# One hybrid-attention encoder block on one core: stores moved to a second DMA queue, one weight load moved forward, filler matmuls redistributed, one bias tile shared

## The chip, the core and the metric

The kernel runs on one core of a Trainium2 chip. A core has TensorE (PE, matrix products), VectorE (DVE), ScalarE (ACT), GpSimd (POOL) and SyncE (SP), each with its own instruction stream that it works off in order, and 16 DMA engines that all of them share. Nearly every DMA here is issued by SP; a few are issued by ACT. The metric is the device time of one execution in microseconds (us). The kernel before takes 1512.31 us, the median of 3 runs that lie between 1511.23 and 1512.66 us.

## The reference

One sequence of 1024 positions with 1024 features goes through one block. What matters here is the mixing part:

```python
h = rmsnorm(x, g_mix[i]) * (1 + scale1) + shift1
proj = h @ w_in[i]
qa, ka, va, qb, kb, vb, ga, gb = jnp.split(proj, split_at, axis=-1)
oa = mixture_of_dilations(heads(qa, N_HEADS_DIL), heads(ka, N_HEADS_DIL), heads(va, N_HEADS_DIL), rel_bias)
ob = neighbourhood_attention_2d(heads(qb, N_HEADS_NA), heads(kb, N_HEADS_NA), heads(vb, N_HEADS_NA), na_rpb[i])
merged = jax.nn.sigmoid(ga) * ya + jax.nn.sigmoid(gb) * yb
```

There are 8 dilated heads (three window patterns, merged by their softmax denominators) and 8 heads of two-dimensional neighbourhood attention on a 16 x 64 grid. A query of the 2-D heads sees 8 rows and 16 columns, with the column window clamped at the edges:

```python
col_start = jnp.clip(cq - NA_COLS // 2, 0, GRID_W - NA_COLS)
bias = rpb[:, (dr + NA_ROWS_MAX - 1)[:, :, None, None], (dc + NA_COLS - 1)[None, None]]
```

The bias depends on the offset between query and key alone. Behind the mixers come the output projection, a gated ConvFFN and a last norm, none of which the change touches.

## The kernel before

Each float32 product is three TensorE products of a high and a low half (`hi`, `lo`). The program runs in stages:

- **Start to about 150 us.** The conditioning vector is multiplied with `w_ada` on VectorE (`row_pairs`, L655), `h` is made, and the value projections are computed for both branches (`v_wide`, L301). In the middle (the `step is None` branch, L728 to L741) the second half of the first query/key pair is projected; `qk_evict` (L372) splits the result into halves (ACT L366, DVE L368 and L370) and stores it to the scratch `q_scr` (L375); `va_chunks` (L412) reorders the values in HBM; `p_load(0)` (L708) fetches the two weight tiles of the first block product; `t_sums` forms operand sums on GpSimd. All this is written in a fixed order.
- **150 to 282 us, the product stage.** Seven pairs of query/key weight tiles go through a seven-product block scheme (`products`, L477; operands from `a_operands`, L428). Every result is split and stored to `q_scr` by `na_evict` (L379) or `qk_evict`: 28 stores of 512 KB. From here on a list scheduler that simulates the engines sets SP's order.
- **282 to 645 us, attention.** A table of slots says what is emitted where. Slots 0 to 63 hold the eight dilated heads (8 slots each), slots 64 to 95 start the eight 2-D heads (4 slots each, one of four blocks of 16 columns per slot, in the order 0, 3, 1, 2). A slot runs output products (`O`), transposes of the probabilities (`T`) and scores (`S`). Between them stand **fills**: a `next` of `fill_steps` (L1287) emits three 128x512 matmuls of the gate projections, which do not depend on attention. `n` of L1337 says how many fills a slot gets; `fill(1)` at L1334 runs ahead of slot 0. PE, ACT and DVE keep the order in which this is written; SP and GpSimd are ordered by the scheduler.
- **From 645 us on.** The rest of the fills, gating, output projection, FFN, final norm.

Names that the steps use: `qk_load` (L395) fetches one head's query and keys (`qs`, `ks`, `kl`) from `q_scr`; `dil_bias` and `bias` (L1212) fetch bias tiles into a ring of 4 buffers, the latter from `na_bias`, whose columns `na_col` holds per column block; `soft` in a head adds the bias and takes the row maximum on DVE (L874, L1237), then ACT takes the exponential (L875, L1239). A pair of dilated heads ends with its denominators: transposed (`turn`, L1113), stored to `st_scr` (`rows`, L1121), reloaded by nine small DMAs (`spread`, L1125 and L1129), and used on DVE (`factors`, L1135). For the last pair this falls into slots 65 to 68.

Of the kernel before, what the change touches and what calls it, by code (L numbers as in the profile page):

```python
# [29 lines left out]
def hybrid_encoder(tc, xT, c, w_ada, small, w_in, p1_bias, p23_bias, na_bias, ln2_mult, ident, w_br, w_out,  # L30
                   w_up, w_down, out):
    nc = tc.nc
    act, dve, pool, pe, sp = nc.scalar, nc.vector, nc.gpsimd, nc.tensor, nc.sync
# [5 lines left out]
    def f(ap):  # L39
        return ap.bitcast(FT)  # L40
# [331 lines left out]
    def qk_evict(pr, y, hf, p, tag):  # L372
        st = qkpool.tile([128, 2, 512], FR, name=tag)
        split_qk(y, (st[:, 0], st[:, 1]), p)
        sp.dma_start(q_scr[pr, 2 * y:2 * y + 2].rearrange("x p s -> p x s")[:, :, halves[hf]], f(st))  # L375

    na_st = {}

    def na_evict(pr, y, hf, p):  # L379
        first = (pr, y) not in na_st  # L380
        if first:
            na_st[pr, y] = [qkpool.tile([128, S], FR, name="qs") for _ in range(2)]
        st = na_st[pr, y]
        if y:
            split_qk(y, [t.rearrange("p (w t r) -> p r w t", w=16, t=16)[:, 2 * hf:2 * hf + 2] for t in st],
                     p.rearrange("p (r w t) -> p r w t", r=2, w=16))
        else:
            for r in range(2):
                split_qk(y, [t.rearrange("p (c w r t) -> p r c w t", c=4, w=16, r=4)[:, 2 * hf + r] for t in st],
                         p.rearrange("p (r w c t) -> p r c w t", r=2, w=16, c=4)[:, r])  # L390
        if not first:
            for x_, t in enumerate(na_st.pop((pr, y))):
                sp.dma_start(q_scr[pr, 2 * y + x_], f(t))

    def qk_load(head):  # L395
        pr, i = divmod(head, 2)
# [127 lines left out]
    with tc.manual_schedule(engines={e.engine for e in (sp, act, dve, pool, pe)}):  # L524
        x = [x_load(0)]
# [201 lines left out]
        for n, step in enumerate(v_steps[:10]):  # L727
            if step is None:  # L728
                for ks in (slice(0, 4), slice(4, 8)):
                    for hv in range(2):  # L730
                        v_split(v_raws[hv], (dve, pool), ks, v_w[hv])
                ps = [ps_g.tile([128, 512], FT, name="pj") for _ in range(2)]
                for k in range(KT):
                    for p, w in zip(ps, qk_w):
                        product(p, w, lambda k: h[1, k], ks=[k])
                for y in range(2):
                    qk_evict(0, y, 1, ps[y], "kl")
                va_chunks(slice(0, 512))
                raw[0] = p_load(0)
                t_sums()  # L740
                prep = [a_operands(raw.pop(0), 4, p_home, p_sts[0], spot=p_spot)]  # L741
            else:
                p = v_wide(*step[1:])
            row_pairs(done_rows, row_ends[n])
            if step is not None:
                for st, pp in zip(step[1:], p):
                    v_out(step[0], st, pp, queue=act)
            done_rows = row_ends[n]
            if n in PREP:
                next(prep[0])  # L750
# [425 lines left out]
                pool.tensor_tensor(dst, dst, src, OP.add)  # L1176
            sp.dma_start(o_scr[0][self.pr], u[1])

    na_col = [0, 576, 1344, 2112]

    class NaHead:
        def __init__(self, head, s0):
# [28 lines left out]

        def bias(self, cb):  # L1212
            kn = 48 * NA_NC[cb]
            bt = self.bt[cb] = sm_pool.tile([128, 896], FT, name="bias", bufs=4)
            sp.dma_start(bt[:, :2 * kn], na_bias[self.head][:, na_col[cb]:na_col[cb] + 2 * kn])

# [114 lines left out]

    att = contextlib.ExitStack()
    att.enter_context(tc.manual_schedule(engines={e.engine for e in (pe, act, dve)}))
    fill(1)  # L1334
    for s in range(102):
        n = 2 + s % 2 if s < 64 else 3 if s < 68 else 2 if s < 96 else 1
        settle()  # L1337
        run(slots[s]["first"])
        run(slots[s]["O"])
# [658 lines left out]
def _na_index():  # L1998
    parts = []
    p = np.arange(128)[:, None]  # L2000
    for cb in range(4):
        n = NA_NC[cb]
        for R in range(2):
            k = np.arange(48 * n)[None, :]
# [65 lines left out]
```

## Time and profile before

| what | value |
|---|---|
| median of 3 runs | 1512.31 us (1511.23 to 1512.66) |
| the profiled execution's own time | 1511.48 us |
| its span, first to last instruction | 1509.7 us |
| PE busy | 1455.2 us (96% of the span) |
| DVE / ACT / POOL busy | 965.4 / 790.3 / 839.3 us |
| mean granted TensorE clock | 0.984 of full |
| DMA moved | 244.28 MB, mean 162 GB/s |

The profile comes from one execution. Its page has the busy time of each engine, the span in 40 slices, the DMA queues, the chain of work that ended last and the costliest groups of instructions; further views of the same trace list waits by releaser, instructions in order of time, and busy times in chosen windows. In a row of the timeline stand start, duration, engine, line, operation, output and inputs, and in brackets how long the engine was idle before it and what released it. Matmuls are pipelined: the time that one costs is the distance between two starts, not its listed duration. An `SPq` or `ACTq` row is a DMA being issued. In a row of windows stand the length, the busy time of PE, PEld (weight load), DVE, ACT and POOL with the number of instructions, the granted TensorE clock, the DMA share and GB/s.

### The profile page before, as it was taken

How to read it: one execution, taken by the hardware profiler on the slowest of the kernel's cores; microseconds unless marked ns; L12 is line 12 of the kernel's file. 1: busy time of each engine (PE TensorE's matmuls, PEld its weight loads, DVE VectorE, ACT ScalarE, POOL GpSimd, SP SyncE). 2: the span in 40 equal slices, each digit the busy share in tenths (PEclk: the TensorE clock that was granted, in tenths of full speed). 3: DMA queues.
4: the chain of work that ended last, by engine and by line, in shares of the span. 5: the costliest groups of instructions: out<-in, count | busy, mean ns of one | idle time of the engine just before them, and what ended most of it. 6: DMA issues, size and time to landing. Idle time of an engine off the chain costs nothing.

```text
span 1509.7 us, 21346 instructions
## 1 busy us (share of the span) xinstructions
PE 1455.2 (96%) x7308; PEld 1228.7 (81%) x7308; DVE 965.4 (64%) x1809; ACT 790.3 (52%) x1479; POOL 839.3 (56%) x690
## 2 busy tenths in 40 slices
PE   9999999799999888999999999999999999999998
PEld 8877888588888777888888878888888888887788
DVE  7695544256666566756634898666666667887865
ACT  6624543177677556764335455444444446574542
POOL 4164675244342245532258848766666676988712
PEclk9999999899999989999999999999999999999999
DMA  9586255776666899958744412222222234632313
GB/s 369 201 311 240 98 181 179 206 187 168 177 182 174 252 218 258 245 192 278 251 131 154 140 56 99 84 84 84 84 84 84 84 119 140 213 125 81 99 49 112
DMA packets 131668, 244.28 MB, mean 162 GB/s; under 512 B 47940, under 2 KB 60868, under 8 KB 131524
## 3 DMA queue, kind: packets, MB, share of 16 engines
q1 hardware_dynamic: 129560, 239.97, 51.3%
q10 hardware_dynamic: 2000, 2.95, 0.5%
q8 instruction: 58, 0.95, 0.3%
q14 instruction: 50, 0.41, 0.1%
HBM read 188.74 MB, written 59.90 MB: 165 GB/s over the span
## 4 chain that ended last, share of the span: by engine, by line
PE 42%; DVE 4%; DMA 4%; POOL 3%; ACT 2%; issue 2%; SPq 0%; DVEq 0%; ACTq 0%; POOLq 0%
PE pj L495 10%; PE pj L496 10%; PE pj L497 10%; PE pj L86 4%; PE pj L84 4%; PE pj L85 4%; DMA oraw<-ob 1%; DMA oraw<-w_ada 1%; DMA wraw<-w_down 1%; POOL wlo L61 1%; POOL wsl L61 1%; ACT op L1518 1%; DVE big L460 0%; POOL big L442 0%; POOL big L441 0%
## 5 line engine op out<-in xcount | busy, mean ns | idle before, releaser
L61 POOL TENSOR_TENSOR wlo<-wraw,whi 128x512 fp32r<-128x512 f32 (+1 forms) x92 | 116.4, 1287 | 130.5 <-ACT whi L57 128.7
L495 PE MATMUL pj<-op,wsh 128*128 128x512 f32 x408 | 158.5, 390 | 1.4 <-ACT wsh L57 1.3
L496 PE MATMUL pj<-op,wsh 128*128 128x512 f32 x408 | 158.7, 389 | 0.4 <-DVE op L1489 0.4
L497 PE MATMUL pj<-op,wsl 128*128 128x512 f32 x408 | 157.3, 389 | 0.0
L61 POOL TENSOR_TENSOR wsl<-big,wsh 128x512 fp32r<-128x512 f32 (+1 forms) x86 | 111.5, 1319 | 44.5 <-ACT wsh L57 39.5
L84 PE MATMUL pj<-h,whi 128*128 128x512 f32 x272 | 118.0, 434 | 0.0
L85 PE MATMUL pj<-h,whi 128*128 128x512 f32 x272 | 109.0, 401 | 0.0
L86 PE MATMUL pj<-h,wlo 128*128 128x512 f32 x272 | 108.9, 400 | 0.0
L1699 DVE SCALAR_TENSOR_TENSOR big<-pj,sm,big 128x512 f32<-128x512 f32 (+2 forms) x183 | 94.9, 563 | 16.5 <-ACT big L1693 15.6
L889 DVE TENSOR_TENSOR tl<-T,th 128x512 fp32r<-128x512 f32 (+3 forms) x120 | 76.5, 650 | 24.9 <-ACT th L885 24.7
L495 PEld LDWEIGHTS pj<-op,wsh 128*128 128x128 f32 x408 | 76.6, 188 | 18.0 <-ACT wsh L57 2.2
L495 PE MATMUL pj<-op,whi 128*128 128x512 f32 x232 | 90.6, 391 | 0.3 <-ACT wc L501 0.3
L496 PE MATMUL pj<-op,whi 128*128 128x512 f32 x232 | 90.5, 390 | 0.2 <-DVE op L1519 0.2
L497 PE MATMUL pj<-op,wlo 128*128 128x512 f32 x232 | 90.3, 389 | 0.0
L496 PEld LDWEIGHTS pj<-op,wsh 128*128 128x128 f32 x408 | 76.6, 188 | 16.6 <-DVE op L1489 0.9
L497 PEld LDWEIGHTS pj<-op,wsl 128*128 128x128 f32 x408 | 76.6, 188 | 16.1 <-POOL wsl L61 0.2
L61 POOL TENSOR_TENSOR wsl<-wraw,wsh 128x384 fp32r<-128x384 f32 (+1 forms) x46 | 56.5, 1250 | 57.5 <-ACT wsh L57 53.2
L874 DVE CUSTOM_DVE_ANT_0 P<-S,bias 128x256 f32<-128x256 f32 x128 | 49.1, 420 | 60.3 <-PE S L1006 32.7
L57 ACT ACTIVATE whi<-wraw 128x1024 fp32r<-128x1024 f32 (+2 forms) x49 | 48.5, 994 | 66.7 <-PE pj L85 30.0
L875 ACT ACTIVATE P<-P,st 128x256 f32<-128x256 f32 x128 | 64.0, 504 | 26.5 <-DVE st L874 26.0
L1693 ACT ACTIVATE big<-pj,sm 128x512 f32<-128x512 f32 x61 | 47.0, 773 | 54.0 <-DVE pj L516 32.1
L516 DVE TENSOR_TENSOR pj<-pj,wc 128x512 f32<-128x512 f32 x40 | 27.8, 695 | 72.1 <-PE pj L497 72.1
(476 smaller groups left out, 4567.1 us busy)
## 6 DMA issues: line engine op xcount, KB each, us to landing
wada<-w_ada SPq DMA_DIRECT2D x31, 512.0 KB
qks<-qs SPq DMA_DIRECT2D x28, 512.0 KB
wraw<-w_in SPq DMA_DIRECT2D x26, 512.0 KB
big<-w_up SPq DMA_DIRECT2D x22, 512.0 KB
wraw<-w_up SPq DMA_DIRECT2D x22, 512.0 KB
big<-as SPq DMA_DIRECT2D x22, 512.0 KB
as<-big SPq DMA_DIRECT2D x21, 512.0 KB
qs<-qks SPq DMA_DIRECT2D x32, 256.0 KB
```

The source lines that it names most:

```text
L57: act.activation(hi, raw, AF.Copy)
L61: lo_eng.tensor_tensor(lo[:, i:i + step], raw[:, i:i + step], f(hi)[:, i:i + step], OP.subtract)
L84: pe.matmul(psum, whi[:, k0 + k], mhi, start=k == 0, stop=False)
L85: pe.matmul(psum, whi[:, k0 + k], mlo, start=False, stop=False)
L86: pe.matmul(psum, wlo[:, k0 + k], mhi, start=False, stop=k == n - 1)
L495: pe.matmul(psum, whi[:, k], bhi, start=j < 4 and k == 0, stop=False, skip_group_check=True)
L496: pe.matmul(psum, whi[:, k], blo, start=False, stop=False, skip_group_check=True)
L497: pe.matmul(psum, wlo[:, k], bhi, start=False, stop=k == n - 1, skip_group_check=True)
L874: dve.tensor_tensor_reduce(pp, d, bias, -1.0, BIG, OP.add, OP.min, mi)
L875: act.activation(pp, pp, AF.Exp, bias=mi, scale=-1.0, accum_out=li)
L889: dve.tensor_tensor(tt[1][:m, :n], pt[:m, :n], f(tt[0])[:m, :n], OP.subtract)
L1699: dve.scalar_tensor_tensor(y[:, dst], src, wt, y[:, dst], OP.mult, OP.add)
```

## The change

Four edits:

1. `qk_evict` and `na_evict` issue their stores to `q_scr` from ACT instead of SP (32 stores).
2. `p_load(0)` stands ahead of the projection, the stores and `va_chunks` in the `step is None` branch, instead of behind them.
3. Fills: 5 instead of 1 ahead of slot 0; slots 0 to 63 get 2, 2, 2, 3 instead of 2, 3, 2, 3; slots 64 to 67 get 2, 3, 2, 3 instead of 3 each; slots 68 to 95 get 2 and 3 in turn instead of 2 each; slots 96 to 101 keep 1. The total is the same (+4, -16, -2, +14).
4. The two middle column blocks (1 and 2) of the 2-D heads share one bias tile: `na_bias` holds three blocks per head, and block 2 uses the tile that was loaded for block 1.

```diff
 def qk_evict(pr, y, hf, p, tag):
-        sp.dma_start(q_scr[pr, 2 * y:2 * y + 2].rearrange("x p s -> p x s")[:, :, halves[hf]], f(st))
+        act.dma_start(q_scr[pr, 2 * y:2 * y + 2].rearrange("x p s -> p x s")[:, :, halves[hf]], f(st))
 def na_evict(pr, y, hf, p):
-                sp.dma_start(q_scr[pr, 2 * y + x_], f(t))
+                act.dma_start(q_scr[pr, 2 * y + x_], f(t))
         v_split(v_raws[hv], (dve, pool), ks, v_w[hv])
+                raw[0] = p_load(0)
                 ps = [ps_g.tile([128, 512], FT, name="pj") for _ in range(2)]
...
                 va_chunks(slice(0, 512))
-                raw[0] = p_load(0)
                 t_sums()
-    na_col = [0, 576, 1344, 2112]
+    na_col = [0, 576, 576, 1344]
 def bias(self, cb):
             kn = 48 * NA_NC[cb]
+            if cb == 2:
+                self.bt[2] = self.bt[1]
+                return
-    fill(1)
+    fill(5)
     for s in range(102):
-        n = 2 + s % 2 if s < 64 else 3 if s < 68 else 2 if s < 96 else 1
+        n = 2 + (s % 4 == 3) if s < 64 else 2 + s % 2 if s < 96 else 1
 def _na_index():
-    for cb in range(4):
+    for cb in (0, 1, 3):
```

How the instructions move is seen best at three places. On SP, where the first block's weights are fetched (`wraw<-w_in`, L713; L375 are the stores of `qk_evict`, L415 and L417 `va_chunks`, L145 the `w_ada` tiles), the difference reads:

```order
 L145 DMA wada<-w_ada 128x1024 x10
-L375 DMA qks<-kl 128x2x512 x2
+L713 DMA wraw<-w_in 128x1024 x2
 L415 DMA v<-v 7x16384 x4
 L417 DMA v<-v 4x8192 x2
-L713 DMA wraw<-w_in 128x1024 x2
 L145 DMA wada<-w_ada 128x1024 x7
```

The weight load stands ahead of the six value DMAs, and the two stores are gone from this queue.

On SP at the end of the product stage, ahead of head 0's query and keys (L401), before:

```order
L65 DMA wraw<-w_in 128x1024 [waits DMAHW4_49,DMAHW2_49,Pool_49]
L375 DMA qks<-qs 128x2x512 [waits DMAHW3_49,DVE_49]
L375 DMA qks<-qs 128x2x512 [waits DVE_49]
L401 DMA qs<-qks 64x1024 [waits DMAHW5_49]
L401 DMA qs<-qks 64x1024 [waits DMAHW6_49]
L401 DMA ks<-qks 64x1024 [waits DMAHW7_49]
L401 DMA ks<-qks 64x1024 [waits DMAHW0_49]
L401 DMA kl<-qks 64x1024 [waits DMAHW1_49,PE_49]
```

and in the change (`DMAHW0` to `DMAHW7` are eight completion counters that the DMAs of both queues take in turn; a DMA waits until the one eight places earlier has landed):

```order
L65 DMA wraw<-w_in 128x1024 [waits DMAHW4_49,DMAHW2_49,Pool_49]
L401 DMA qs<-qks 64x1024 [waits DMAHW5_49]
L401 DMA qs<-qks 64x1024 [waits DMAHW6_49]
L401 DMA ks<-qks 64x1024 [waits DMAHW7_49,DVE_49]
L401 DMA ks<-qks 64x1024 [waits DMAHW0_49]
L401 DMA kl<-qks 64x1024 [waits DMAHW1_49,PE_49]
L401 DMA kl<-qks 64x1024 [waits DMAHW2_49]
L848 DMA lnm<-ln2_mult 128x384 [waits DMAHW3_49,PE_49]
L691 DMA bias<-p_bias 128x512 [waits DMAHW4_49,PE_49]
```

The two last stores are not ahead of the loads any more. They stand on ACT, each behind the split that it stores (L366), with a wait for DVE's half; L949 is the split of the next fill weights:

```order
L366 ACTIVATE qs<-pj 128x512 [waits DMAHW3_49,PE_49]
L949 ACTIVATE whi<-wraw 128x512 [waits DMAHW4_49]
L949 ACTIVATE whi<-wraw 128x512
L375 DMA qks<-qs 128x2x512 [waits DVE_49]
L366 ACTIVATE qs<-pj 128x512 [waits DMAHW5_49,DVE_49]
L375 DMA qks<-qs 128x2x512 [waits DVE_49]
L366 ACTIVATE qs<-pj 128x512 [waits DMAHW6_49,DVE_49]
L375 DMA qks<-qs 128x2x512 [waits DVE_49]
```

On SP at the start of the 2-D heads, where the last pair's denominators go out (L1121) and come back (L1125, L1129), before:

```order
L1215 DMA bias<-na_bias 128x576 [waits DMAHW0_49,DVE_49]
L1121 DMA sts<-fr 64x128 [waits DMAHW1_49,DVE_49]
L1307 DMA gs<-gs 128x512 [waits DMAHW2_49,Activation_49]
L1125 DMA fs<-sts 64x2x32 [waits DMAHW3_49,DMAHW1_49]
```

and in the change:

```order
L1218 DMA bias<-na_bias 128x768 [waits DMAHW6_49,DVE_49]
L1121 DMA sts<-fr 64x128 [waits DMAHW7_49,DVE_49]
L401 DMA ks<-qks 64x1024 [waits DMAHW0_49,PE_49]
L401 DMA qs<-qks 64x1024 [waits DMAHW1_49,PE_49]
L401 DMA qs<-qks 64x1024 [waits DMAHW2_49]
L1125 DMA fs<-sts 64x2x32 [waits DMAHW7_49,DMAHW3_49]
```

Three loads of a later head's query and keys, 256 KB each, now stand between the store and the reload.

## The prediction

> **What bounds the kernel now.** I read the busy times by stage first, then TensorE's waits by releaser, then the timelines around the longest of them. PE is busy 96% of the span, so only its idle time and its slow clock can be won. By stage (product stage and what precedes it, change to attention, dilated slots, 2-D slots):
>
> ```profile
> 95.00:282.00 187.00, 182.77 (x803) 149.99 (x802) 99.60 (x138) 75.05 (x118) 115.01 (x83) 0.99 0.51 182
> 282.00:300.00 18.00, 7.43 (x27) 5.77 (x26) 2.25 (x9) 3.61 (x11) 4.68 (x6) 0.62 0.99 246
> 300.00:506.00 206.00, 202.17 (x1271) 179.58 (x1270) 124.38 (x389) 145.25 (x400) 80.96 (x76) 1.00 0.71 187
> 506.00:645.00 139.00, 119.48 (x721) 105.48 (x720) 88.44 (x269) 87.74 (x238) 68.59 (x61) 0.91 0.94 236
> ```
>
> PE idles 4.2 us in the first, 10.6 in the second, 3.8 in the third (DVE and ACT are busy 60% and 71% there, so PE sets the pace), and 19.5 in the fourth, where the clock is also 0.91 and the DMA engines are full. These 38 us and some 9 us of slow clock (an estimate: about 1.5 to 2 us behind each of five long waits, as worked out below) are all that the four edits can reach; the instructions behind slot 95 keep their order. TensorE's waits:
>
> ```profile
> PE T L1256 <- DVE stb L1244: 12.8, 13, 4.9
> PE S L1005 <- DMA ks<-qks: 8.8, 1, 8.8
> PE T L1021 <- DVE tl L889: 2.9, 5, 0.7
> PE pv L308 <- ACT vs L315: 2.5, 1, 2.5
> PE S L1006 <- DMA kl<-qks: 1.8, 1, 1.8
> ```
>
> **The change, part by part.** The sum is made against the profiled execution, 1511.5 us, which is 0.8 below the median.
>
> *Weights sooner.* The 2.5 us wait of L308 is ACT's doing: ACT stands at L57, waiting for the first block's weights, with the eviction L315 queued behind it.
>
> ```profile
> 95.78 2.88 DVE L61 TENSOR_TENSOR vwl<-wraw,vwh 128x512 fp32r<-128x512 f32 x1
> 108.55 1.85 SPq L713 DMA_DIRECT2D wraw<-w_in  x2
> 121.57 1.06 ACT L57 ACTIVATE whi<-wraw 128x1024 fp32r<-128x1024 f32 x1 [12.01 <-DMA wraw<-w_in]
> 125.00:130.00 5.00, 5.00 (x17) 3.97 (x16) 0.69 (x1) 2.60 (x3) 5.00 (x5) 0.69 0.91 347
> ```
>
> The load goes out at 108.55 and lands 13 us later, behind two stores and six value DMAs. In the change it needs only its buffers; the second is free when DVE's split ends at 98.66. Ten us earlier and ahead of the value DMAs, it lands near 110 at the latest, before ACT needs it. The 2.5 us go, and with them the clock dip after it: 0.69 over 5 us is 1.5 us. Term: **-4.0** (bounds -4.0 and 0, the latter if ACT is held at the same place by something else). A stall of 2.5 us lowered the clock here. The Trainium skill (TensorE: Matmul & The Clock Gate, section "Why this matters for your kernels") says to avoid idle gaps over about 3 us; by that rule a 2.5 us gap would cost nothing more and the sum would be 1.5 us smaller; the trace disagrees, and the row decides.
>
> *Stores on ACT.* One issue costs ACT 0.33 us:
>
> ```profile
> 107.17 0.33 ACTq L316 DMA_DIRECT2D vbc<-vs  x1
> ```
>
> 32 of them are 11 us, plus each time the wait for DVE's half (0.69 us when DVE is free, L370 in the next fence): some 33 us on ACT between 58 and 285 us. ACT is busy 75 of the 187 us from 95 on, so this fits; queued behind a waiting store are the next eviction and weight split, needed by PE a whole block product later. Term: **0**, covered by ACT's 112 idle us; without that cover it would be a rival (below).
>
> *Start of attention.* PE stands 8.8 + 1.8 us for head 0's keys.
>
> ```profile
> 278.71 0.35 SPq L65 DMA_DIRECT2D wraw<-w_in  x1
> 279.80 0.69 DVE L370 TENSOR_TENSOR qs<-pj,qs 128x512 fp32r<-128x512 f32 x1 [0.71 <-ACT qs L366]
> 280.52 3.08 SPq L375 DMA_DIRECT2D qks<-qs  x2
> 283.65 1.33 SPq L401 DMA_DIRECT2D qs<-qks  x2
> 295.32 1.01 POOL L852 TENSOR_TENSOR bias<-bias,lnm 128x384 f32<-128x384 f32 x1 [16.64 <-DMA bias<-p_bias]
> 295.00:300.00 5.00, 5.00 (x20) 4.10 (x19) 1.55 (x8) 3.12 (x10) 4.68 (x6) 0.62 1.03 213
> 299.61 0.60 PE L1021 MATMUL T<-idt,P 128*128 128x128 f32 x4
> ```
>
> Today the loads leave at 283.65, behind two stores that wait for DVE. In the change they follow the weight load of 278.71, so query and first keys leave at about 279.1: 4.5 us sooner. Their 1.0 MB, the 0.5 MB of weights and half a store take some 6.5 us at the 246 GB/s of this stage: landing near 286 instead of 291.2. PE has 4 more fills until then (4 x 0.69 = 2.7 us, priced below), from 282.4 to 285.1, so most of this wait is covered. Next late is the bias: its DMA waits for the last store to land (eight places earlier), so it leaves near 286.5 and lands near 292 to 293, against 295; DVE and ACT then need 3 us, and PE stands again, at the first transposes, about 3.5 us and with a slow clock after. That transpose moves from 299.6 to about 296; I take off 0.6 for the clock. Term: **-3** (bounds -1: only the bias's 1.5 us with some clock lost; -6: all of the keys' 5.2 us and the clock kept). The Trainium skill (DMA: Bandwidth & Descriptors, "Issuing engines are not separate DMA queues") says that a second issuing engine saves only issuing time; by it this term would be the 1 us bound and the total 2 us higher. What I count is SP's blocked issue, not bandwidth.
>
> *Dilated slots.* A fill's three matmuls, and the distances between the score products of slots 62 to 64:
>
> ```profile
> 503.97 0.39 PE L84 MATMUL pj<-h,whi 128*128 128x512 f32 x1
> ...
> 504.66 0.22 PE L1086 MATMUL O<-th,vv 128*128 128x128 f32 x1
> 499.81 0.28 PE L1048 MATMUL S<-ks,qb 128*128 128x256 f32 x1
> 502.58 0.28 PE L1048 MATMUL S<-ks,qb 128*128 128x256 f32 x1
> 506.26 0.29 PE L1227 MATMUL S<-ks,qs 128*128 128x288 f32 x1
> ```
>
> A fill costs 0.69 us. Slots with two fills already run without a wait (2.77 us at 499.81), so sixteen fewer are worth 16 x 0.69 = 11.0. Where three light slots follow one another, ACT (145.25 us over 62 slots, 2.3 a slot) comes near their 2.8 us, and the 0.7 us waits of L1021 can grow: I give back 1.5. Term: **-9.5** (bounds -7 and -11).
>
> *2-D slots.* Three long stalls, and the steady cycle of four slots (618.05 to 633.46, one head):
>
> ```profile
> 528.33 1.06 PE L1256 MATMUL T<-idt,P 128*96 128x128 f32 x4 [6.53 <-DVE tl L889]
> 546.53 1.06 PE L1256 MATMUL T<-idt,P 128*96 128x128 f32 x4 [4.91 <-DVE stb L1244]
> 583.59 1.06 PE L1256 MATMUL T<-idt,P 128*96 128x128 f32 x4 [3.92 <-DVE stb L1244]
> 618.05 0.29 PE L1227 MATMUL S<-ks,qs 128*128 128x288 f32 x1
> 633.46 0.29 PE L1227 MATMUL S<-ks,qs 128*128 128x288 f32 x1
> 525.50 0.18 DVE L1135 TENSOR_TENSOR fl<-fs 64x32 f32<-64x32 f32 x1 [6.80 <-DMA fs<-sts]
> 535.90 0.56 DVE L1237 CUSTOM_DVE_ANT_0 P<-S,bias 128x384 f32<-128x384 f32 x1 [1.65 <-PE S L1227]
> 544.74 0.56 DVE L1237 CUSTOM_DVE_ANT_0 P<-S,bias 128x384 f32<-128x384 f32 x1 [6.12 <-DMA bias<-na_bias]
> 574.70 0.55 DVE L1237 CUSTOM_DVE_ANT_0 P<-S,bias 128x384 f32<-128x384 f32 x1
> 581.80 0.56 DVE L1237 CUSTOM_DVE_ANT_0 P<-S,bias 128x384 f32<-128x384 f32 x1 [4.39 <-DMA bias<-na_bias]
> 513.42 0.47 SPq L1121 DMA_DIRECT2D sts<-fr  x1
> ```
>
> The stalls at 546 and 583 are DVE waiting for a bias. Only blocks 1 and 2 are 384 wide; 535.90 is block 1 of the second head, so 544.74 is block 2: exactly the load that is dropped. The same holds for 574.70 and 581.80, two heads on. That is 4.9 + 3.9 us, and behind each the slow clock (four transposes take 1.06 us there against 0.60 at 299.61), for which I take the 1.9 us that 5 us at 0.62 lose in the row from 295: 12.6 in all. Eight loads of 384 KB go, 3.1 MB of 139 us x 236 GB/s = 32.8 MB, 13 us of DMA time. With the queue full another transfer will be late in places: I give back 3. The stall at 528 is the reload of the denominators, 12 us after their store went out; it stays. PE reaches it 0.7 us sooner (slot 66 loses a fill), and three loads stand in between, which SP can issue while it waits anyway: +1.0. Slots 64 to 67 lose two fills, -1.4. The 14 added fills are 9.7 us; odd slots are followed by a short wait (the 12.8 us of the first wait row less its two long ones leave 4.0 for eleven, 0.36 each), which hides 14 x 0.36 = 5.0: +4.7. Term: -12.6 + 3 + 1.0 - 1.4 + 4.7 = **-5.3** (bounds -10 with no new lateness and full cover, +7 with none of the bias gain kept).
>
> Sum: -4.0 + 0 - 3 - 9.5 - 5.3 = -21.8, so 1489.7 for an execution like the profiled one, **1490** for the median.
>
> **Rivals.** *The transfers stay the bound of the 2-D slots*: the dropped bias was only the visible end of a full queue, and the next head's bias or keys come late instead. The DMA share of 0.94 speaks for it; against it, from 595 us on the same transfers run without a long stall. The 9.6 us that I keep of the 12.6 return and the added fills find no wait to hide in (5.0): 1505. *All of it goes*: the dilated slots give the full 11 (1.5 more), nothing new is late in the 2-D slots (3), the start gives 6 (3): 1482.5. *The dilated slots are not bound by PE*: the fills leave holes and are paid in full later, 9.5 + 5.0 us, and 3 us of bias stall remain: about 1508. The 2.77 us slots speak against it. *ACT becomes the bound of the product stage*, the slower side: SP spent long waits at these stores,
>
> ```profile
> SPq L375 <- DVE qs L368: 26.1, 6, 9.0
> SPq L375 <- DVE qs L370: 14.7, 6, 6.0
> SPq L375 <- DVE kl L370: 8.8, 1, 8.8
> ```
>
> 49.6 us for DVE. If ACT inherits them, its weight splits (L57) come late and PE waits for them. It decides from 22 of these 49.6 us reaching PE; at 30 the time is 1520. Against it: SP waited because it arrived early, while ACT arrives right after its own half.
>
> **How the numbers follow.** Forecast 0.55 (its own range 1483 to 1497), transfers stay the bound 0.20, all of it goes 0.13, dilated slots not bound 0.06, ACT the bound 0.06. The likeliest is 1490. The range goes down to 1479, a little below the second-best case, and up to 1506, which takes in the first rival. A measurement of this kernel tells 0.2%, 3 us, from no change. Faster 0.91 (the first three cases and half of the fourth), same 0.03, slower 0.06.
>
> **What would show it.** No wait of L308 near 121 us, and the clock at 1.00 behind it. L401 issued ahead of the last L375, the first score product before 288. Dilated slots of 2.7 to 3.0 us three times out of four. No wait of L1237 for `na_bias` over 3 us, but one of L1135 for `fs`. A 2-D head of about 16.0 us in the steady part instead of 15.4. The prediction is wrong if PE waits for L57 splits between 150 and 280 us, if the 2-D slots still hold 15 us of idle PE, or if the dilated slots show as much idle time as fills were taken out.

## The result

The changed kernel takes 1502.16 us (median of 4 runs, 1500.23 to 1503.85) against 1512.49 for the kernel before on the same chip: a ratio of 0.9929, 95% interval 0.9910 to 0.9947, some 11 us faster. A second measurement on another chip (x15 below) gives 0.9922 (0.9906 to 0.9938). The forecast was 22 us faster, 1490. The change helps, by half of what was forecast, and the time lies nearest to the first rival (transfers stay the bound of the 2-D slots, 1505).

Busy time by stage in the changed kernel, with the same stages as in the prediction, each about where it lies now (columns: PE, PEld, DVE, ACT, POOL, granted clock, DMA share, GB/s):

```profile
93.70:281.00 187.30, 185.18 (x821) 152.14 (x819) 100.39 (x139) 76.53 (x118) 116.11 (x83) 1.00 0.53 188
281.00:297.00 16.00, 7.16 (x22) 5.54 (x23) 1.47 (x8) 3.18 (x10) 5.44 (x6) 0.66 0.82 247
297.00:493.00 196.00, 193.26 (x1223) 171.75 (x1222) 121.87 (x389) 144.07 (x401) 79.55 (x75) 0.99 0.73 188
493.00:632.00 139.00, 119.64 (x737) 105.55 (x735) 88.57 (x266) 86.41 (x234) 69.75 (x61) 0.95 0.90 224
```

The product stage is full, the dilated slots are ten microseconds shorter, and the 2-D slots still idle 19 of 139 us. TensorE's longest waits:

```profile
PE T L1259 <- DVE tl L889: 13.9, 4, 12.4
PE S L1005 <- DMA ks<-qks: 4.4, 1, 4.4
PE T L1259 <- DVE stb L1247: 3.7, 6, 1.8
PE T L1021 <- ACT P L875: 2.3, 2, 2.2
```

(From L1215 on, a line of the changed kernel is three higher than before.) The two bias waits of 4.9 and 3.9 us are gone, and so is L308's. In their place one wait of 12.4 us stands at the first row, where 6.5 stood. Between the first score product of slot 64 and that of slot 94, before and now:

```profile
506.26:640.93 134.67, 115.15 (x692) 101.41 (x690) 85.49 (x261) 84.66 (x229) 67.41 (x60) 0.91 0.95 237
```

```profile
493.55:630.33 136.78, 117.42 (x724) 103.61 (x723) 87.52 (x260) 84.74 (x230) 68.64 (x61) 0.95 0.91 224
```

This stretch got 2.1 us longer. With these marks the 9.1 us between the two profiled executions split as follows.

| part | forecast | measured | from |
|---|---|---|---|
| weights sooner | -4.0 | -4.4 | first fill ahead of slot 0 at 280.91, now 276.54 |
| start of attention | -3 | +1.5 | slot 2 scores at 300.74, now 297.87 (-2.9), less the -4.4 |
| dilated slots 2 to 63 | -9.5 | -9.8 | slot 64 scores at 506.26, now 493.55 (-12.7), less the -2.9 |
| 2-D slots | -5.3 | +2.1 | the two rows above |
| all behind slot 94 | 0 | +1.5 | span less 640.93 or 630.33; one fill more, 0.7, stands here now |

The starts come from one execution of each kernel. In that of x15, the same changed kernel again, the five parts are -5.5, +0.1, -9.1, +0.8 and +1.6 us, so one part is known to some 1.5 us.

The weights have landed by 108.43, as forecast (what ends the wait of L57 there is a value DMA), and the clock behind the old stall is full:

```profile
93.12 5.38 SPq L713 DMA_DIRECT2D wraw<-w_in  x2
108.43 1.06 ACT L57 ACTIVATE whi<-wraw 128x1024 fp32r<-128x1024 f32 x1 [3.94 <-DMA v<-v]
125.00:130.00 5.00, 5.00 (x24) 4.14 (x23) 4.79 (x8) 2.50 (x4) 3.80 (x3) 1.00 0.70 234
```

The start of attention, SP's waits between 278 and 292 us first, then its timeline and TensorE's:

```profile
SPq L848 <- DMA qks<-qs: 3.6, 1, 3.6
SPq L691 <- DMA qks<-qs: 3.6, 1, 3.6
```

```profile
275.44 1.15 SPq L401 DMA_DIRECT2D qs<-qks  x2
284.15 0.33 SPq L848 DMA_DIRECT2D lnm<-ln_mult  x1
288.17 0.33 SPq L691 DMA_DIRECT2D bias<-p_bias  x1
285.23 0.55 PE L1005 MATMUL S<-ks,qs 128*128 128x256 f32 x1 [4.44 <-DMA ks<-qks]
288.06 0.55 PE L1006 MATMUL S<-kl,qs 128*128 128x256 f32 x1 [2.28 <-DMA kl<-qks]
295.62 0.33 PE L1021 MATMUL T<-idt,P 128*128 128x128 f32 x1 [2.17 <-ACT P L875]
```

The loads leave 8.2 us sooner than before, 4.4 of it the weights' doing, but SP then stands twice, 7.2 us in all, for ScalarE's stores to land (each issue waits for the transfer eight places earlier). The bias therefore leaves only at 288.17, and the transposes wait for what follows it.

The 2-D entry, from the timelines of DVE, SP and PE in order of time, and two windows:

```profile
498.42 0.28 DVE L1120 COPY fr<-T 64x128 f32<-64x128 f32 x1
504.59 0.47 SPq L1121 DMA_DIRECT2D sts<-fr  x1
512.86 0.61 SPq L1125 DMA_DIRECT2D fs<-sts  x1
517.72 0.18 DVE L1135 TENSOR_TENSOR fl<-fs 64x32 f32<-64x32 f32 x1 [13.12 <-DMA fs<-sts]
520.56 1.06 PE L1259 MATMUL T<-idt,P 128*96 128x128 f32 x4 [12.38 <-DVE tl L889]
515.00:520.00 5.00, 0.00 (x0) 0.00 (x0) 2.19 (x9) 1.72 (x5) 0.00 (x0) 0.50 0.51 109
520.00:525.00 5.00, 4.44 (x15) 3.86 (x16) 4.86 (x9) 3.25 (x10) 3.73 (x4) 0.50 1.09 234
```

The statistics of the last dilated pair are ready at 498.7. They leave 5.9 us later, have landed at 512.9, are back at 517.7, and DVE, which works in order, stands at L1135 all that while with TensorE behind it. Before, the statistics left 1.4 us behind their copy.

The two halves of this round trip differ. From the store's issue to that of the reload, and from there to L1135:

```profile
504.59:512.86 8.27, 3.35 (x21) 2.48 (x19) 0.00 (x1) 0.99 (x3) 1.11 (x1) 0.91 1.05 291
512.86:517.72 4.86, 0.00 (x0) 0.00 (x0) 0.00 (x1) 0.00 (x0) 0.00 (x0) 0.50 0.16 34
```

While the store is on its way the DMA engines are full. During the reload they are nearly empty (share 0.16, 34 GB/s): SP stood at L1125 until the store had landed and issued nothing else, and then issues nine small DMAs for some 3.5 us. This second half takes the same 4.7 to 4.9 us in the kernel before, the change, x3, x9 and x11, at a share of 0.05 to 0.16 (x4 is the exception, 7.2 us at 0.53). So bytes can set only the first half there, and the round trip itself keeps the DMA engines from moving bytes for some five microseconds.

### The profile page after: what moved, and what is told of

It reads as the page before. It is cut to its first block, busy times and chain, and to the rows that moved or that the text cites. A ratio compares the mean times of both kernels' runs of the same rounds, so it can differ in the third digit from the quotient of the medians.

```text
span 1500.6 us, 21335 instructions
## 1 busy us (share of the span) xinstructions
PE 1451.0 (97%) x7308; PEld 1225.1 (82%) x7308; DVE 967.5 (64%) x1809; ACT 790.4 (53%) x1479; POOL 839.4 (56%) x690
## 4 chain that ended last, share of the span: by engine, by line
PE 67%; DMA 9%; DVE 8%; POOL 6%; ACT 5%; issue 3%; SPq 1%; ACTq 0%; DVEq 0%; POOLq 0%
PE pj L497 13%; PE pj L495 13%; PE pj L496 13%; PE pj L84 6%; PE pj L86 6%; PE pj L85 6%; PE T L1021 1%; PE O L1033 1%; POOL wlo L61 1%; DMA oraw<-ob 1%; POOL wsl L61 1%; DMA wraw<-w_down 1%; DMA oraw<-w_ada 1%; PE T L1069 1%; DMA ks<-qks 1%
## 5 line engine op out<-in xcount | busy, mean ns | idle before, releaser
L85 PE MATMUL pj<-h,whi 128*128 128x512 f32 x272 | 108.4, 399 | 0.0
L57 ACT ACTIVATE whi<-wraw 128x1024 fp32r<-128x1024 f32 (+2 forms) x49 | 48.5, 994 | 57.7 <-PE pj L85 28.9
L1250 POOL TENSOR_SCALAR P<-P,stb 128x288 f32<-128x288 f32 (+1 forms) x32 | 41.2, 1286 | 65.4 <-DVE stb L1247 28.1
```

The lines of the kernel that those rows point to most:

```text
L57: act.activation(hi, raw, AF.Copy)
L85: pe.matmul(psum, whi[:, k0 + k], mlo, start=False, stop=False)
```

## The experiments

Times differ by a few microseconds from chip to chip, so kernels are compared by their ratio to the kernel before on the same chip; "-11" means that ratio less one, times 1512 us. "The stretch" is the time from slot 64's first score product to slot 94's, in one profiled execution (that of x6 is its fastest, 1489.7 us with a median of 1494.3). It holds 75 fills in the change and in every run that keeps its table of fills, 64 in the kernel before, x3 and x10, and 68 in x11 to x14; a fill is 0.69 us of TensorE, so stretches compare directly only at the same number. x5 to x9 and x12 do not give the reference's output and serve for their times alone.

| run | ratio (95% interval) | us | stretch | wait for denominators |
|---|---|---|---|---|
| the change | 0.9929 (0.9910 to 0.9947) | -11 | 136.8 | 12.4 |
| x15 the change again | 0.9922 (0.9906 to 0.9938) | -12 | 135.5 | 12.1 |
| x1 factors later | 0.9909 (0.9893 to 0.9925) | -14 | 134.2 | under 1 |
| x2 store on ScalarE | 0.9924 (0.9905 to 0.9943) | -11 | 136.6 | 5.2 |
| x3 old fills | 0.9926 (0.9910 to 0.9941) | -11 | 130.2 | 6.3 |
| x4 bias apart | 0.9931 (0.9911 to 0.9950) | -10 | 141.8 | 11.6 |
| x5 less bias | 0.9914 (0.9898 to 0.9930) | -13 | 134.5 | 12.3 |
| x6 no reload | 0.9889 (0.9873 to 0.9905) | -17 | 127.6 | none |
| x7 no reload, less bias | 0.9848 (0.9833 to 0.9862) | -23 | 125.6 | none |
| x8 factors later, less bias | 0.9854 (0.9838 to 0.9871) | -22 | 127.1 | under 2 |
| x9 copies sooner | 0.9916 (0.9892 to 0.9939) | -13 | 133.9 | 5.9 |
| x10 two edits | 0.9942 (0.9923 to 0.9961) | -9 | 133.3 | 8.1 |
| x11 fills at the turn | 0.9872 (0.9849 to 0.9895) | -19 | 125.7 | 4.1 |
| x12 three together | 0.9889 (0.9867 to 0.9912) | -17 | 126.3 | under 2 |
| x13 turn, bias apart | 0.9941 (0.9926 to 0.9955) | -9 | 136.1 | 4.0 |
| x14 turn, factors later | 0.9898 (0.9882 to 0.9914) | -15 | 127.4 | under 2 |

**x1, factors three slots later.** Does it pay to take the long wait away?

```diff
-            at(s0 + 20, "last", self.factors)
-            at(s0 + 21, "last", self.shares)
+            d = 3 if pr == 3 else 0
+            at(s0 + 20 + d, "last", self.factors)
+            at(s0 + 21 + d, "last", self.shares)
```

(and `load`, `weigh` and `merge` likewise)

> The changed kernel with one edit: for the last pair of dilated heads the DVE work that needs the reloaded denominators (factors, shares, and all that follows them) stands three slots later; their store and reload keep their places. Theory 1 (latency: the changed kernel's 12.4 us wait of TensorE at 520.6 us is DVE standing in order at L1135 for a reload that comes late, and the transfers as such have room): with three more slots, some 11 us, the reload is there first, the wait at 520.6 goes down to under 3 us and with it the slow clock behind it (0.50 at 515 to 525, some 3 us), and nothing of the size takes its place: 1502.2 - 10 - 3 = about 1489. Theory 2 (throughput: the queue is the bound of the 2-D slots, and the place where TensorE stands for it is incidental): the wait moves to the keys or a bias of the next heads, the total of TensorE's idle time from 506 to 640 stays at about 20 us, and the time stays at 1500 to 1503.

Measured: -14, 2 us better than the change, within the intervals of both. The 12.4 us are gone and the stretch is 2.6 us shorter, not 13: a new wait stands at 548, where ScalarE waits for values issued behind the stores of the factors (timelines of SP, ACT and PE).

```profile
541.30 2.01 SPq L773 DMA_DIRECT2D vv<-v  x4
545.31 0.42 ACT L779 ACTIVATE vv<-vv 96x256 fp32r<-96x256 f32 x1 [6.20 <-DMA vv<-v]
548.40 1.06 PE L1260 MATMUL T<-idt,P 128*96 128x128 f32 x4 [5.30 <-DVE tl L889]
```

The first theory, that only the round trip counts, falls; the time itself is a little under what the second allowed.

**x2, the store of the statistics on ScalarE's queue.** Was the store late because it stood behind seven other issues on SP?

```diff
-            sp.dma_start(st_scr[self.pr], rows)
+            act.dma_start(st_scr[self.pr], rows)
```

> The changed kernel with one edit: the store of the softmax statistics, L1121, is issued by ScalarE instead of SyncE, for all four pairs. In the changed kernel its data are ready at 498.7, SyncE issues it at 504.6 behind seven loads, and it has landed at 512.9, when the reload leaves. Theory 1a (the place in SyncE's order): the store leaves near 499.5; SyncE reaches the reload near 508, and as the reload still stands behind the loads already sent, the wait of 12.4 us shrinks by 3 to 5 us with 1 us of clock: about 1497. Theory 1b (backlog of the queue as a whole: wherever it is issued, the store lands only when the 2 MB sent before it have moved): the store still lands near 510 to 512, the wait shrinks by at most 2 us: 1500 to 1502. Theory 2 (throughput): under 1 us of difference in time, whatever the wait does.

The store left at the same moment, 504.58 (504.59 in the change), 6.6 us behind its copy (5.9 in the change), and now ScalarE stood for it; its timeline:

```profile
504.58 0.45 ACTq L1121 DMA_DIRECT2D sts<-fr  x1
505.08 0.59 ACT L934 ACTIVATE u<-O 64x512 f32<-64x512 f32 x1 [6.98 <-DMA ks<-qks]
```

The releaser is a load of keys issued before it. So the store does not wait for its turn on one engine: it waits for an earlier transfer to land, whichever engine issues it. Theory 1b, the backlog, holds, and 1a falls. The wait at the denominators fell to 5.2 us because TensorE was already held 5.1 us at 507, through DVE, by the ScalarE that stood for the store (the two add up to 10.3), and the denominators were back 1.5 us sooner. Time: no difference from the change that can be told. The Trainium skill (DMA: Bandwidth & Descriptors, "Issuing engines are not separate DMA queues") says that issuing from a second engine saves only the issuing time; this run agrees (504.58 against 504.59).

**x3, the old fills,** and **x4, separate biases:** each takes one edit back.

```diff
-    fill(5)
-        n = 2 + (s % 4 == 3) if s < 64 else 2 + s % 2 if s < 96 else 1
+    fill(1)
+        n = 2 + s % 2 if s < 64 else 3 if s < 68 else 2 if s < 96 else 1
```

> The changed kernel with the table of fills of the kernel before (three edits left: stores on ScalarE, weights sooner, one bias for both middle blocks). SyncE's order is then nearly that of the kernel before: behind the store of the statistics stands the reload, ahead of the next head's queries and keys. Theory 1 (the lengthened stall is a matter of order, which the fills shifted): the 2-D slots keep a stall of 6 to 7 us for the denominators and lose the two bias stalls, so they are 8 to 12 us shorter than before; the dilated slots are as long as before: about 1512.5 - 4 (weights) - 2 (start) - 10 = 1496 to 1499. Theory 2 (one bias saves nothing, as the queue is the bound): 2-D slots as before, about 1506. Rival 3 (sharing the bias itself makes the stall: the shared buffer is held longer and the third bias load, ahead of the store, waits for a buffer): stall of 11 to 13 us, about 1501 to 1503.

```diff
-    na_col = [0, 576, 576, 1344]
+    na_col = [0, 576, 1344, 2112]
-            if cb == 2:
-                self.bt[2] = self.bt[1]
-                return
```

(and the layout of `na_bias` in four parts)

> The changed kernel with four biases a head again (the other three edits left). It prices the shared bias under the changed table of fills. Forecast of the prediction: -12.6 us of two bias stalls, 3 given back: without it the time is about 10 us longer, 1512. Theory 1: the same, as the bias loads come back on top of a stall for the denominators that stays at 11 to 13 us: 1508 to 1513. Theory 2 (throughput): eight loads of 384 KB are 3.1 MB, 13 us of transfer time at 236 GB/s, so 1512 to 1515. Rival 3 (sharing makes the long stall): the stall falls back to about 7 us and the sum is within 3 us of the changed kernel: 1500 to 1505.

Neither differs from the change by more than the intervals (-11 and -10 against -11 and -12). Both miss what theories 1 and 2 expected; x4's time lies where only rival 3 had put it, but not for its reason, as the stall did not fall back. In x3 the wait is as short as before, so sharing the bias does not make it, and rival 3 falls; the fills do. The copy and the return in x3, from DVE's timeline:

```profile
505.16 0.27 DVE L1120 COPY fr<-T 64x128 f32<-64x128 f32 x1
518.67 0.18 DVE L1135 TENSOR_TENSOR fl<-fs 64x32 f32<-64x32 f32 x1 [6.54 <-DMA fs<-sts]
```

Its statistics are ready 6.7 us later than in the change, and back only 1.0 us later. What the lighter dilated slots win, TensorE waits away at this place. In x4 the long wait stays (11.6 us) and DVE waits for two biases again:

```profile
508.28 0.56 DVE L1237 CUSTOM_DVE_ANT_0 P<-S,bias 128x384 f32<-128x384 f32 x1 [5.57 <-DMA bias<-na_bias]
573.78 0.56 DVE L1237 CUSTOM_DVE_ANT_0 P<-S,bias 128x384 f32<-128x384 f32 x1 [4.29 <-DMA bias<-na_bias]
```

The first stands just ahead of the long wait and costs TensorE 1.9 us, the second 3.9. Its stretch is 5.0 us longer, but the median does not show it.

**x5 to x8: two limits.** One edit takes bytes away: heads 2 to 7 use the biases of head 1.

```diff
+            if self.head > 1:
+                self.bt[cb] = bias_1[min(cb, 1) if cb < 3 else 3]
+                return
```

The other takes the round trip away:

```diff
         def spread(self):
             self.fs = at_pool.tile([64, 4, 32], FT, name="fs", bufs=1)
+            if self.pr == 3:
+                pool.memset(self.fs, 1.0)
+                return
```

x7 has both, x8 the first and the later factors of x1.

> The changed kernel, but the 2-D heads 2 to 7 use the bias tiles of head 1 instead of loading their own (their output is then not the reference's): 18 loads, 5.9 MB, 23 us of the queue's time at 250 GB/s, all behind the long wait of the changed kernel, and SyncE's order up to that wait as it was. Theory 2 (throughput: what the 2-D slots do not get is bytes): the later waits, 6.6 us in sum from 528 us on, go, and the queue empties early enough that the time falls by 6 to 9 us: 1493 to 1496. Theory 1 (latency: only the 12.4 us wait for the denominators counts, and it stays): 1499 to 1502, the 2-D slots 64 to 94 at 133 to 136 us against 136.8.

> The changed kernel, but for the last pair of dilated heads the reloaded denominators are replaced by ones set in place on GpSimd (the store stays, the output of that pair is not the reference's); so nothing in the 2-D slots waits for the store to land and the reload. Theory 1 (latency): the 12.4 us wait and the slow clock behind it go and nothing replaces them: 1502.2 - 12 - 3 = 1487, slots 64 to 94 in 122 to 124 us. Theory 2 (throughput): as with the later factors, where only 2.6 us of the stretch from slot 64 to 94 were won (136.8 to 134.2), waits for keys, V or biases of some 8 us come in its place: 1496 to 1499, slots 64 to 94 in 131 to 135 us.

> Both of the two: ones in place of the last pair's reloaded denominators, and the biases of head 1 for heads 2 to 7 (output not the reference's). Theory 1: as without the reload alone, 1486 to 1487, since bytes do not count. Theory 2: only now does the stretch from slot 64 to 94 come to its cost on TensorE, some 122 us (four slots of 4.37, 3.69, 4.14 and 4.02 us a head): 1485 to 1488, some 10 us below the run without the reload alone. A mixture would stand between: 1490 without the reload, 1486 with both.

> The kernel with the last pair's factors three slots later (1498.4 us) and the biases of head 1 for heads 2 to 7. In that kernel a wait of 5.3 us stands at 548 and one of 2.5 at 568, where V of the next head was issued behind the eight stores of factors (7.1 us of issuing). Theory 2 (throughput): these waits go with the 5.9 MB: 1498.4 - 8 - 2 of clock = 1487 to 1490. Rival 4 (SyncE's order alone: whatever stands behind the factors' stores is late): they stay, 1495 to 1498.

Measured, with the change (x15) at -12: less bias -13, no reload -17, both -23; factors later -14, with less bias -22. 5.9 MB less is worth 1 us where the round trip stands (x5, between the two theories' figures, so it decides nothing alone), 6 where it is gone (x6 to x7) and 8 where its users come later (x1 to x8). Each limit hides the other. Taking the reload away also spares the queue the five microseconds in which SP stands and the reload runs alone, so it lifts a part of the limit in bytes too; how much of the 5 us of x6 that is was not tried apart. Both theories were half right: with one limit lifted some 1 to 5 us are won, with both 10 to 11, and the stretch is shorter than the 129.4 us (134.7 - 5.3) that the prediction came to. Rival 4 of x8 falls.

**x9, the copies of V sooner.** Does more time for the same bytes shorten the round trip?

```diff
-    for n, cb in zip((54, 56, 59, 61), (0, 3, 1, 2)):
+    for n, cb in zip((52, 53, 55, 57), (0, 3, 1, 2)):
```

> The changed kernel with the sixteen copies that lay out V for the 2-D heads (L422, 3.6 MB) in slots 52, 53, 55 and 57 instead of 54, 56, 59 and 61, where the queue still has room (share 0.59 at 460 to 470). In the changed kernel the store of the statistics left at 504.6, 5.9 us behind its data, because each issue waits for the transfer eight places earlier to land; issued by ScalarE it left at the same 504.6. Theory 5 (backlog: the dilated slots got shorter, the bytes ahead of the store did not, so the round trip returns when the bytes allow and the earlier arrival of TensorE is handed back): with 2 to 4 slots, 6 to 11 us, more for the same bytes the store leaves within 3 us of its data, the wait of 12.4 us falls to 5 to 8 us, slots 64 to 94 to 131 to 133 us, the time to 1495 to 1498. Theory 1 (the round trip itself, 8.3 us to land and 4.9 us of reload, not what stands ahead of it): the wait stays over 10 us, 1500 to 1502.

The copies reuse the scratch of the dilated heads' V and come too early for it here, so the output of x9 and of x12 is not the reference's, against what x12's expectation says of it. The store left 0.6 us behind its copy (499.88 to 500.45), the wait fell to 5.9 us and the stretch to 133.9: the mechanism shows as theory 5 said. The time, -13, cannot be told from the change's and misses the range of theory 5: slot 64 came 1.2 us later and waits of 3.3 and 2.1 us followed.

**x10, the first two edits alone** (old fills and separate biases, the diffs of x3 and x4 together).

> Only the first two edits (stores on ScalarE, weights sooner) on the kernel before; fills and biases as before. It closes the square with old fills (1500.8), separate biases (1502.1) and the whole change. Terms of the prediction: -4.0 and -3, so 1503.7 by these alone. If fills and bias each were worth what they show alone and added up, the square would give the change as the sum; as separate biases cost the change nothing that can be told (1502.1) and old fills neither (1500.8), theory 5 (two limits, of which each edit lifts one) expects the two edits alone at 1504 to 1507, fills alone worth 2 to 5, the bias alone 4 to 6, and both together no more than the larger of the two. If the two edits alone give 1501 or less, fills and bias together are worth nothing.

-9, where the prediction's two terms give -7. Fills and shared bias, forecast at -14.8 together, so add 2 to 3 us to it; the shared bias alone 2 (x3), the fills alone 2 (x4), each within the uncertainty and the bias below the 4 to 6 expected.

**x11, ten fills at the turn.** If TensorE arrives early for nothing, work put there should be free.

```diff
-        n = 2 + (s % 4 == 3) if s < 64 else 2 + s % 2 if s < 96 else 1
+        n = 2 + (s % 4 == 3) if s < 54 else 3 if s < 69 else 2 if s < 89 else 2 + s % 2 if s < 96 else 1
```

> The changed kernel with ten fills moved: three a slot in 54 to 68, two in 69 to 88 (the dilated slots before 54 as in the change, the sum of fills as before). Theory 5 (backlog): between 54 and 68 TensorE has nothing to gain from arriving early, as the round trip returns when the bytes allow; fills are free there, and each odd slot from 69 to 87 is 0.4 us shorter: the wait falls from 12.4 to 5 to 7 us, the later slots win 10 x 0.4 to 0.7: 1495 to 1498. Theory 1 (the wait follows the store, and the store follows TensorE): with fills the store is later as well, the wait stays over 10 us, and only the later slots win: 1498 to 1501.

-19: better than both kernels, 8 us below the change. DVE, SP and PE around the round trip, and the stretch:

```profile
503.69 0.27 DVE L1120 COPY fr<-T 64x128 f32<-64x128 f32 x1
503.99 0.47 SPq L1121 DMA_DIRECT2D sts<-fr  x1
510.22 0.62 SPq L1125 DMA_DIRECT2D fs<-sts  x1
514.94 0.18 DVE L1135 TENSOR_TENSOR fl<-fs 64x32 f32<-64x32 f32 x1 [4.79 <-DMA fs<-sts]
518.04 1.06 PE L1259 MATMUL T<-idt,P 128*96 128x128 f32 x4 [4.09 <-DVE tl L889]
497.11:622.79 125.68, 113.44 (x704) 100.25 (x702) 85.13 (x260) 85.04 (x229) 68.47 (x61) 0.97 0.95 234
```

Of the 11.1 us by which the stretch is shorter than the change's, seven fills that now stand ahead of slot 64 make some 4.8, and slot 64 comes 3.6 us later for them; the rest goes with TensorE's waits, of which those over 1 us sum to 7.8 us against 16.7. The statistics are ready 5.3 us later than in the change (503.69 against 498.42), the store leaves at once and still 0.6 us sooner than the change's, and DVE goes on 2.8 us sooner. Theory 1, by which the store follows TensorE, falls. That the store lands in 6.2 us instead of 8.3 goes with SP's order (in the change three loads of 256 KB are issued between the store and the reload, here one load of weights); that this is the cause was not tried, and x9, with no load between, took 6.8.

**x12, three together** (x1, x9 and x11), and **x14, x11 with the later factors.**

> The changed kernel with three edits that keep the output: the last pair's factors three slots later, the copies of V sooner, and the ten fills moved to slots 54 to 68. By theory 5 the wait for the denominators is gone (their users stand three slots later and the store leaves sooner) and the later V loads have a lead: TensorE's waits over 1 us between slots 64 and 94 sum to under 6 us, slots 64 to 94 in 125 to 130 us and the time 1488 to 1493. If the bytes of the 2-D slots bind however they are ordered, 1495 to 1498, as with the later factors alone.

> The kernel with ten fills moved to slots 54 to 68, and the last pair's factors three slots later. The wait for the denominators there is 4.1 us, with 2.75 us of another behind it, and 12.2 us of idle time in all between slots 64 and 94. Theory 5: the 4.1 us go, with 1 to 2 us of slow clock, but as the bytes bind as well some waits of 2 to 5 us come later: 1490 to 1495. If the round trip was the whole of what is left: 1488 to 1490.

-17 and -15, not better than x11 alone. In x14 a wait of 4.7 us at 561 comes for the 4.1 that go; x12 has one of 4.2. Both lie above the range that theory 5 expected (x12 in that of a bound by bytes). What waiting is left in x11 these edits only move. x11 is the best version found that keeps the output.

**x13, x11 with separate biases.** Does the shared bias pay where TensorE is on time?

> The kernel with ten fills moved to slots 54 to 68 (0.9872 of the time before), with four biases a head again. Theory 5 (two limits): with TensorE on time at the round trip, the 3.1 MB of the shared bias show: the bias stalls of the kernel before come back at one or two heads, 4 us each with some slow clock, and the time is 4 to 9 us longer, 1498 to 1503. If the shared bias is worth nothing in any place, as under the changed table of fills: within 3 us of 1494.

-9: without the shared bias ten of x11's 19 us are lost (the intervals 0.9926 to 0.9955 and 0.9849 to 0.9895 do not touch). The bias waits are back: three of over 3 us on DVE, where x11 has one (3.9 us at 545). The first two:

```profile
524.57 0.56 DVE L1237 CUSTOM_DVE_ANT_0 P<-S,bias 128x384 f32<-128x384 f32 x1 [3.77 <-DMA bias<-na_bias]
536.19 0.46 DVE L1237 CUSTOM_DVE_ANT_0 P<-S,bias 128x288 f32<-128x288 f32 x1 [5.84 <-DMA bias<-na_bias]
```

**x15, the change again,** beside x13 and x14.

> The changed kernel itself, on the same chip as the two: 0.993 of the time before (0.991 to 0.9947), some 8 us above the kernel with ten fills moved.

As expected. Four kernels now form a square of two edits, all with the reference's output:

| | change's fills | fills at the turn |
|---|---|---|
| separate biases | -10 (x4) | -9 (x13) |
| shared bias | -11, -12 | -19 (x11) |

Neither edit alone moves the time by more than the intervals; both together win 9 us. The squares of x5 to x8 have the same form.

## Why the prediction was right or wrong

**What bounds the kernel now:** right on the places (start, transition, 2-D slots), wrong in reading each idle interval as a separate sum that can be won by itself.

**Weights sooner:** right, -4.4 for -4.0. L57 has its weights at 108.4 and L308 waits no more.

**Stores on ACT at 0:** right between 93.7 and 281 us: PE idles 2.1 of 187 us, and none of its waits there is for a split of L57. The rival (ACT becomes the bound) fell.

**Start of attention:** wrong, -3 forecast, +1.5 measured (+0.1 in x15's execution); with the old fills it is -1.2 in x10 and -1.0 in x3, each from its own first fill. Two steps failed. "Landing near 286": the loads left within a microsecond of the forecast, seen from the first fill, but the first scores started 3.6 us later than that (285.23, plus the 4.4 us by which everything here is sooner, against 286). The bytes named there, at 246 GB/s, already make 7.1 us and not "some 6.5"; ScalarE issued two stores at 276.11 and 278.83, beside these loads, but that they took the rest was not tried. And "its DMA waits for the last store to land ..., so it leaves near 286.5": SP waited for two stores, 3.6 us each, and the bias left at 292.6 on that scale. So the fills taken to be covered here were not: three more stand ahead of slot 2, 2.1 us. Moving a store to another engine's queue freed SP's next issue, but not the counters that both share. The rule of the Trainium skill that the prediction quotes gave a term of -1, nearer than mine.

**Dilated slots:** right, -9.8 for -9.5. Slots with two fills now follow each other at 2.67 us:

```profile
484.45 0.28 PE L1048 MATMUL S<-ks,qb 128*128 128x256 f32 x1
487.12 0.28 PE L1048 MATMUL S<-ks,qb 128*128 128x256 f32 x1
```

**2-D slots:** here the forecast failed most. Of the 12.7 us between the forecast and the measured difference of the profiled executions 7.4 lie here (4.5 at the start, 1.5 behind slot 94; the other two parts take 0.7 off). The first two heads take 2.4 us longer than before, where by the prediction's terms the first bias stall should have gone; the five behind them take 0.4 us less. By its own terms:

- The loads named as the cause of the bias waits were the right ones, and no wait of L1240 for `na_bias` over 3 us is left. But "-12.6 + 3" assumed that the saving stands by itself. Under the change's fills it cannot be told from nothing (x4), under fills that keep TensorE on time it is about 10 us (x13 to x11). In x4 both bias waits are there on DVE, and one of them falls just ahead of the long wait.
- "The stall at 528 ... stays ... +1.0" is the step with the largest miss: 6.5 became 12.4 us, and the clock behind it 0.50 from 515 to 525. I moved TensorE's arrival forward by what slot 66 loses, 0.7 us, and forgot the 9.5 us that the dilated slots had just won: the statistics were ready 13 us sooner, and the transfers ahead of their store were not. The return of the denominators moved by 7.8 us, from 525.5 to 517.7, the arrival of TensorE by 13.6. That the store is what was held, by what is launched from slot 54 on, x9 shows (5.9 behind the copy became 0.6), and that the earlier arrival is what lengthened the wait, x3 and x11.
- The added fills cost about what was forecast, but not evenly. Heads 2 to 6 took 84.8 us before, 3.9 of it the bias wait, and take 84.4 with ten fills more. That is 0.35 us a fill, 0.54 if the 1.9 us of slow clock behind that wait are taken off as well; 0.34 was forecast. The head that took 15.4 us in the prediction takes 16.4 (16.0 forecast):

```profile
606.24 0.29 PE L1230 MATMUL S<-ks,qs 128*128 128x288 f32 x1
622.68 0.29 PE L1230 MATMUL S<-ks,qs 128*128 128x288 f32 x1
```

The head ahead of it takes 17.8, with a wait of 1.4 us for GpSimd, which is still splitting the weights of the next fills (L950; 0.4 us before).

**The signs to look for** were all met for the first three stages, and in the 2-D slots the waits for `na_bias` went and that for `fs` stayed, and so was the sign of being wrong: "if the 2-D slots still hold 15 us of idle PE". They hold 19.

**The rivals:** "the transfers stay the bound of the 2-D slots", at 0.20, has the nearest time, 1505, in part by luck: what it said would come late, the next head's bias or keys, did not (no such wait over 2 us is left in the change), and its sentence against ("from 595 us on the same transfers run without a long stall") was true as well. What neither had is that the round trip and the transfers cover each other.

## What to carry to other kernels

Before adding up the idle intervals of a profile, ask for each what sets the moment at which the awaited thing comes: where that moment is set by transfers, work won ahead of it only makes the wait longer, and where two such limits hide each other they show in full only when lifted together. A store and reload through HBM at the change from a light to a full queue is such a place; giving the engine that would wait there independent work (ten fills) won 8 us here, where issuing the store from another engine won nothing. Look at both halves of it: here the store went out into a full queue, while the reload ran in an almost empty one, and a reload in fewer DMAs, or loads issued ahead of it, was not tried. And test an edit that "does nothing" together with the one that may hide it: the shared bias was worth nothing that could be told in one order of fills and ten microseconds in the other.

## What the runs showed of the hardware

Over the stretch from slot 64 to 94 the granted clock was 0.95 with the wait of 12.4 us (the row in the result) and 0.99 with no wait over 2.6 us (x7, where waits of 1.9 and 2.5 us fall into the second row):

```profile
489.14:614.78 125.64, 116.53 (x724) 102.98 (x723) 88.02 (x260) 84.78 (x230) 68.84 (x61) 0.99 0.83 200
...
500.00:520.00 20.00, 14.42 (x81) 12.07 (x80) 13.78 (x36) 10.86 (x29) 10.18 (x9) 0.91 0.93 229
```

The Trainium skill (TensorE: Matmul & The Clock Gate, "Why this matters for your kernels") warns of idle gaps over about 3 us. The long wait agrees, with 0.50 in the ten microseconds around its end. Shorter waits cost clock in one place and not in the other: of the 20 us in the second row, the ten with the wait of 1.9 us (3.0 us idle in all) had 0.83, the ten with that of 2.5 us had 1.00, and before the change 0.69 stood behind 2.5 us.

A DMA issue that waits blocks the engine it stands on, compute included: ScalarE stood 6.98 us at one store in x2, and TensorE 5.1 us behind it.

A store of 32 KB took 7.2 us from its issue to that of the reload before, 8.3 in the change, 6.8 in x9 and 6.2 in x11, with a DMA share of 0.82 to 1.05 meanwhile. At the 280, 291, 264 and 285 GB/s of these stretches some 2.0, 2.4, 1.8 and 1.8 MB moved in that time (an estimate from the rows); whether it is the bytes ahead of a small transfer that set its time was not tried by itself.
